# First FFN of a two-layer hybrid block on one core: the first tokens are transposed before they are normalised, and the token factor is applied later

## The chip, the core and the metric

The kernel runs on one core of a Trainium2 chip. The metric is the device time of one execution in microseconds (us), as the median of several runs. A core has five engines that run in parallel, each through its own list of instructions in a fixed order: TensorE (PE in the profile, its weight loads PEld), VectorE (DVE), ScalarE (ACT), GpSimd (POOL) and SyncE (SP), which here issues all DMA transfers. They wait for one another by semaphores. Matrix products land in PSUM, everything else lives in SBUF, and weights come from HBM.

## What is computed

The reference takes `x` (256 tokens of 1024 channels, float32) through two layers. Each layer has a feed-forward block at half weight, a mixer (a convolution with a state-space part, or attention) and another feed-forward block, each between two RMS norms. Only the beginning matters here:

```python
def rms_norm(x, g):
    y = x * lax.rsqrt(jnp.mean(x * x, axis=-1, keepdims=True) + NORM_EPS)
    return y * g

def swiglu(u, w1, w2):
    gate, up = jnp.split(u @ w1, 2, axis=-1)       # w1: 1024 x 5632
    return (jax.nn.silu(gate) * up) @ w2           # w2: 2816 x 1024

h = x
h = h + 0.5 * rms_norm(swiglu(rms_norm(h, g[0]), ffn_w1[0, 0], ffn_w2[0, 0]), g[1])
```

An RMS norm multiplies each token by one number (the token factor, from the mean square of its 1024 channels) and each channel by one weight (the norm weight `g`). Since both are plain factors, `(r * x * g) @ w` equals `r * ((x * g) @ w)` for each token.

## The kernel before, in words

**Precision by parts.** A float32 value is split into a high part, rounded to the type `fp32r`, which PE multiplies fast, and a low part, the remainder. A product of two such values is three PE products: high by high, high by low, low by high (`mm3`, line 646). Splitting takes one ScalarE instruction (the copy that rounds) and one VectorE instruction (the subtraction); weights are split on the chip too (`split`, line 613, and `prefetch`, line 617). In the profile `raw` is a weight unit as it was loaded (128 x 2048, 1 MB), `wh` and `wl` are its high and low part, made in pieces of 512 columns. Four units of each have room.

**The work of a feed-forward block** (`ffn`, line 830). The 2816 hidden channels are taken in 11 chunks of 256. The first two chunks are computed token-major (`gated_tok`, line 774): tokens are the rows of the result, so for each block of 128 tokens (t = 0, 1) the stationary side is x and the moving side 512 columns of weights (256 of the gate, 256 of the up half). The gate is then applied (`gate_mul`, line 803), and the hidden values are transposed. Chunks 2 to 10 are computed feature-major (`gated_feat`, line 811, with `by_parts`, line 682): here the stationary side is a block of weights and the moving side is the transposed x with all 256 tokens, high and low parts in one go. For both, x has to lie transposed in SBUF, channels on partitions, in eight blocks of 128 channels (`kb`). Between these, products with `w2` (`down`, line 846) are accumulated; those of chunks 0 and 1 stand behind chunk 2. A chunk of two units of weights takes PE 10.9 us.

**The beginning** (`run`, line 1356). SP loads the first token block in two halves, then an identity matrix, the first norm weights, the second token block in two halves, and weights. For each token block `post_pre` (line 738) takes the squares' sums on ScalarE, the token factor by `rstd` (line 726: VectorE and a power on GpSimd), multiplies the tokens by it on VectorE (`y` in the profile), transposes the result in eight 128 x 128 pieces on PE (`to_transposed`, line 704), and splits it while it copies it out of PSUM, where the norm weight is applied as well, which then stands one to a partition: four ScalarE copies with a scale, then four VectorE instructions for the low parts. The transposed x lies in the tiles `x`.

**What sets the order.** All instructions are first recorded (`Recorder`, line 252), each with a rank: its number in the recording, plus an offset (`moved`, line 315: -2000 for `post_pre`, -1950 for the splits of the first two weight units, +800 for later ones). Each carries what it depends on; of a PSUM tile the recorder also makes an instruction of one engine depend on the last user on another engine (`add`, line 277). `schedule` (line 340) then plays the program through with estimated costs and landing times, and takes on each engine, among the instructions that could start next, the one with the lowest rank. The order so found is written down, one list for each engine, and line 475 issues it: this is why nearly every row of the profile carries the line L475. On the chip the order is fixed; an engine waits at each instruction until its inputs are there.

PSUM has eight banks: four `a`, two `w`, one `t` and one `c`. Buffers in SBUF are named `s`, `cv`, `pt`, `sg`, `x` and so on, each with a fixed number of places.

Of the kernel before, what the change touches and what calls it, by code (L numbers as in the profile page):

```python
# [17 lines left out]
P = 128  # L18
D = 1024
DFF = 2816  # L20
SEQ = 256
NT = SEQ // P
KB = D // P
EPS = 1e-6
# [7 lines left out]
HURRY = 2000  # L32
# [130 lines left out]
N_CHAN = 340  # L163
# [86 lines left out]
class Recorder:  # L250
# [26 lines left out]
    def add(self, engine, name, args, kw):  # L277
        op = Op(len(self.ops), engine, name, args, kw)
        op.rank = op.index + self.offset
        self.ops.append(op)  # L280
        out = kw.get("out", args[0] if args else None)
        writes = (out, kw.get("accum_out"))
        views = [a for a in (*args, *kw.values()) if isinstance(a, View)]
        for a in sorted(views, key=lambda a: a in writes):
            self.touch(op, a, a in writes)
        for buf in op.bufs:
            if buf.kind.psum:
                own = engine in ("tensor", "vector") and any(w.buf is buf for w in writes if isinstance(w, View))
# [4 lines left out]
        op.cost, op.tail = cost(op, out)  # L293

    def touch(self, op, view, write):
        buf = view.buf
# [17 lines left out]
    @contextmanager  # L314
    def moved(self, ranks):

        before = self.offset
        self.offset += ranks
        yield
        self.offset = before  # L320

    @contextmanager
    def together(self):
# [16 lines left out]
    def schedule(self):  # L340
# [51 lines left out]
        while len(order) < len(ops):  # L392
# [9 lines left out]
            for b in o.bufs:  # L402
                if b.slot is None:
# [7 lines left out]
                    left[b] = len(b.uses)  # L411
                    b.last = 0.0
            length = o.cost
            if e == "scalar" and o.table:
                if o.table != table:
                    length += TABLE_LOAD
                table = o.table
# [64 lines left out]
GAP = 100.0  # L482
PAIRED = True
FIRST = 730.0
DMA_START = 1100.0
DMA_LATENCY = 900.0
LOOK = {"tensor": 50.0, "vector": 100.0, "scalar": 100.0, "gpsimd": 0.0, "sync": 0.0}
# [67 lines left out]
class Kernel:  # L555
    def __init__(self, ctx, tc, x, weights, w_dt, gains, chan, heads, dt_bias, consts, out):
        self.tc, self.nc = tc, Recorder(tc)
        self.weights, self.gains = weights, gains
        self.x, self.out = x, out
        self.n = 0  # L560
        self.next_unit = 0
        self.use_unit = 0
        self.units = {}
        self.bg = []
# [12 lines left out]
        self.ident = self.keep("ident", [P, P])  # L577
        self.order = self.keep("order", [P, 2, P])
# [4 lines left out]
        self.mean = self.keep("mean", [P, P])  # L583
        nc.gpsimd.memset(self.mean, 1.0 / D)
# [26 lines left out]


    def split(self, hi, lo, src, engine=None):
        self.nc.scalar.activation(hi, src, AF.Copy)
        (engine or self.nc.vector).tensor_tensor(out=lo, in0=src, in1=hi.bitcast(F32), op=ALU.subtract)

    def prefetch(self, upto):
# [36 lines left out]
        return [self.slot([P, 2, 2, SEQ], F32R, "x") for _ in range(KB // 2)]  # L654

    def xa(self, xT, t, kb):
        return tuple(xT[kb // 2][:, kb % 2, p, t * P : (t + 1) * P] for p in range(2))

    def xb(self, xT, kb):
# [114 lines left out]
    def gated_tok(self, xT, func, consume, bank="tt", first=False):  # L774
        nc = self.nc
        units = [[self.unit(512), self.unit(512)] for _ in range(2)]
        prods = {}
# [1 line left out]
        def product(t, c):  # L779
            ps = self.ps([P, 512])  # L780
            self.tok_major(ps, xT, t, units[c])
            prods[t, c] = self.gate_mul(ps, func)

        if first:
            ps = [self.ps([P, 512]) for _ in range(NT)]
            for part in range(2):
                for t in range(NT):
                    self.tok_major(ps[t], xT, t, units[0], range(part * 4, part * 4 + 4))
            for t in range(NT):
                prods[t, 0] = self.gate_mul(ps[t], func)  # L790
        else:
            product(0, 0)
        product(0, 1)
# [9 lines left out]
    def gate_mul(self, ps, func, out=None):  # L803
        if out is None:
            out = self.slot([P, 256], tag="pt")
        sg = self.slot([P, 256], tag="sg")
        self.nc.scalar.activation(sg, ps[:, 0:256], func)
        self.nc.vector.tensor_tensor(out=out, in0=sg, in1=ps[:, 256:512], op=ALU.mult)
        return out

    def gated_feat(self, xT, func, parts=None):
# [15 lines left out]
        return out  # L827


    def ffn(self, xT, done):  # L830
        nc = self.nc
        hid = {}

# [522 lines left out]
    def run(self):  # L1356
# [5 lines left out]
            (self.attention, False),  # L1362
            (self.ffn, True),
        ]
        xT = self.transposed_tile()
        load = self.nc.sync.dma_start
        for hf in range(2):
            c = slice(hf * 512, (hf + 1) * 512)
            load(out=self.h[0][:, c], in_=self.x[0:P, c])
        load(out=self.ident, in_=self.consts[:, C_ID : C_ID + P])  # L1370
        load(out=self.gain0, in_=self.in_small[0][:, N_CHAN : N_CHAN + KB])
        for hf in range(2):
            c = slice(hf * 512, (hf + 1) * 512)
            load(out=self.h[1][:, c], in_=self.x[P : 2 * P, c])
        self.prefetch(2)
        for t in range(NT):
            self.post_pre(t, None, False, None, self.gain0, xT)
        for i, (stage, half) in enumerate(stages):
            box = {}

# [8 lines left out]
            stage(xT, done)  # L1389
            xT = box["x"]  # L1390
        self.nc.issue()

# [44 lines left out]
```

## Time and profile before

| | before |
|---|---|
| median of 3 runs | 1077.49 us (1076.29 to 1078.73) |
| profiled execution, first to last instruction | 1074.9 us (its time is given by this span alone) |
| granted PE clock, mean | 0.998 |
| PE busy | 1058.9 us |
| VectorE busy | 762.3 us |
| ScalarE busy | 654.9 us |
| first weight piece landed | 8.23 us |
| first product of the first chunk | 9.20 us |

How to read it: times count from the first instruction of the profile. A row of the timeline gives start, duration, engine, line, operation, the tile written, an arrow and the tiles read, shapes, the number of merged instructions and, in brackets, how long the engine had been idle and what ended it. PE's records overlap, as one product starts before the one ahead has drained; the pace is read from the starts, not the durations. In the list of groups the second number behind the bar is the mean duration of one in ns. For DMA issues the last number is the time from issue to landing.

### The profile page before, as it was taken

How to read it: one execution, taken by the hardware profiler on the slowest of the kernel's cores; microseconds unless marked ns; L12 is line 12 of the kernel's file. 1: busy time of each engine (PE TensorE's matmuls, PEld its weight loads, DVE VectorE, ACT ScalarE, POOL GpSimd, SP SyncE). 2: the span in 40 equal slices, each digit the busy share in tenths (PEclk: the TensorE clock that was granted, in tenths of full speed). 3: DMA queues.
4: the chain of work that ended last, by engine and by line, in shares of the span. 5: the costliest groups of instructions: out<-in, count | busy, mean ns of one | idle time of the engine just before them, and what ended most of it. 6: DMA issues, size and time to landing. Idle time of an engine off the chain costs nothing.

```text
span 1074.9 us, 15876 instructions
## 1 busy us (share of the span) xinstructions
PE 1058.9 (99%) x5822; PEld 897.9 (84%) x5822; DVE 762.3 (71%) x1572; ACT 654.9 (61%) x1449; POOL 147.4 (14%) x140
## 2 busy tenths in 40 slices
PE   7999999999999999999999999999999999999997
PEld 5888888888878888888888888888888788888886
DVE  5756666799999885666677666668688868566663
ACT  7745555777776664655565646556576656465552
POOL 2000000169896000000000000000000500000000
PEclk9999999999999999999999999999999999999999
DMA  9765564545324575546537465454645235554621
GB/s 335 282 214 180 181 211 181 170 145 197 118 90 148 194 264 205 193 164 225 181 138 275 162 229 182 171 196 155 252 155 186 99 118 207 205 196 162 227 82 39
DMA packets 30638, 196.58 MB, mean 183 GB/s; under 512 B 3680, under 2 KB 4576, under 8 KB 8032
## 3 DMA queue, kind: packets, MB, share of 16 engines
q1 hardware_dynamic: 30560, 195.57, 51.9%
q8 instruction: 45, 0.74, 0.3%
q14 instruction: 33, 0.27, 0.1%
HBM read 194.51 MB, written 1.05 MB: 182 GB/s over the span
## 4 chain that ended last, share of the span: by engine, by line
PE 93%; DVE 3%; ACT 2%; DMA 0%; issue 0%; SPq 0%; DVEq 0%; POOLq 0%; POOL 0%; ACTq 0%
PE w L475 38%; PE a L475 32%; PE t L475 12%; PE c L475 12%; DVE c L475 2%; DVE t L475 1%; ACT wh L475 1%; DMA raw<-in_weights 0%; ACT junk L475 0%; DVE s L475 0%; ACT c L475 0%; ACT t L475 0%; SPq L475 0%; DVE m L475 0%; DVE h L475 0%
## 5 line engine op out<-in xcount | busy, mean ns | idle before, releaser
L475 DVE TENSOR_TENSOR wl<-raw,wh 128x512 fp32r<-128x512 f32 x640 | 411.4, 690 | 157.2 <-ACT wh L475 155.0
L475 ACT ACTIVATE wh<-raw 128x512 fp32r<-128x512 f32 x712 | 403.9, 625 | 194.8 <-PE a L475 78.9
L475 PE MATMUL w<-x,wh 128*128 128x512 f32 (+1 forms) x864 | 263.8, 364 | 0.9 <-DVE pt L475 0.7
L475 PE MATMUL a<-wh,s 128*128 128x512 f32 x800 | 253.0, 390 | 0.0
L475 PE MATMUL w<-x,wl 128*128 128x256 f32 x752 | 209.2, 278 | 0.0
L475 PEld LDWEIGHTS w<-x,wh 128*128 128x128 f32 x864 | 154.7, 188 | 28.2 <-DVE pt L475 1.0
L475 PEld LDWEIGHTS a<-wh,s 128*128 128x128 f32 x800 | 149.9, 188 | 33.2 <-ACT s L475 1.0
L475 PE MATMUL w<-wh,x 128*128 128x512 f32 x512 | 166.8, 400 | 1.0 <-ACT x L475 0.8
L475 PE MATMUL a<-wl,s 128*128 128x512 f32 x400 | 156.5, 391 | 0.0
L475 PEld LDWEIGHTS w<-x,wl 128*128 128x128 f32 x752 | 141.4, 188 | 1.9 <-issue 0.9
L475 POOL TENSOR_TENSOR m<-m,mhalf 128x1 f32<-128x1 f32 x28 | 18.1, 647 | 794.8 <-DVE m L475 794.7
L475 PE MATMUL t<-x,wh 128*128 128x512 f32 x336 | 117.1, 390 | 0.0
L475 PE MATMUL c<-x,wh 128*128 128x512 f32 x336 | 117.1, 390 | 0.0
L475 PEld LDWEIGHTS w<-wh,x 128*128 128x128 f32 x512 | 95.9, 189 | 21.6 <-ACT x L475 1.6
L475 PE MATMUL w<-wl,x 128*128 128x512 f32 x256 | 101.8, 400 | 0.0
L475 POOL TENSOR_TENSOR wl<-raw,wh 128x512 fp32r<-128x512 f32 x72 | 90.6, 1293 | 28.0 <-ACT wh L475 27.9
L475 PE MATMUL t<-x,wl 128*128 128x256 f32 x336 | 93.2, 277 | 0.0
L475 PE MATMUL c<-x,wl 128*128 128x256 f32 x336 | 93.1, 277 | 0.0
L475 PEld LDWEIGHTS a<-wl,s 128*128 128x128 f32 x400 | 75.1, 188 | 14.3
L475 DVE TENSOR_TENSOR sg<-w,sg 128x256 f32<-128x256 f32 x72 | 30.5, 424 | 75.4 <-ACT sg L475 74.1
L475 ACT ACTIVATE sg<-w 128x256 f32<-128x256 f32 x96 | 36.6, 382 | 77.0 <-PE w L475 77.0
L475 PEld LDWEIGHTS c<-x,wh 128*128 128x128 f32 x336 | 63.1, 188 | 13.5
(176 smaller groups left out, 1201.3 us busy)
## 6 DMA issues: line engine op xcount, KB each, us to landing
raw<-in_weights SPq DMA_DIRECT2D x176, 1024.0 KB, 4.8
g<-in_gains SPq DMA_DIRECT2D x11, 512.0 KB, 5.5
raw<-in_weights SPq DMA_DIRECT2D x8, 256.0 KB, 6.3
h<-in_x SPq DMA_DIRECT2D x4, 256.0 KB, 3.1
out<-h SPq DMA_DIRECT2D x4, 256.0 KB, 2.0
g<-in_consts SPq DMA_DIRECT2D x3, 192.0 KB, 2.3
chan<-in_chan SPq DMA_DIRECT2D x1, 170.0 KB, 8.7
order<-in_consts SPq DMA_DIRECT2D x1, 128.0 KB, 8.8
```

The lines of the kernel that those rows point to most:

```text
L475: o.ins = f(*[real(a) for a in o.args], **{k: real(a) for k, a in o.kw.items()})
```

## The change

The beginning of the kernel is rewritten; behind the first feed-forward block nothing differs.

- The identity is no longer loaded. GpSimd makes it (a clear, then a select on the diagonal). SP's order is now: first token block, norm weights, second token block, weights.
- PE runs four throw-away f32 products of the identity with itself, and then turns the raw tokens by f32 products with the identity, eight for each token block.
- The turned raw tokens are multiplied by the norm weights as they are copied out of PSUM and split into high and low parts, for the first four channel blocks of each token block by ScalarE, for the other four by one VectorE product. The token factor isn't in them. The second token block's parts depend, for the scheduler, on the first split of a weight piece.
- The two token-major chunks use these parts. Their gate applies the token factor: as a scale of the activation, and in the VectorE product.
- Behind these two chunks `scaled` makes the x for all others: each block's token factor is widened to 128 x 128 (ScalarE), turned by PE, copied out (ScalarE); VectorE adds high and low part, multiplies by the factors, and the result is split anew.
- The sums of squares move behind; they depend, for the scheduler, on the first load or on the fourth split.
- The scheduler counts PE instructions that start ahead of 6500 ns at twice their cost.

```diff
     def split(self, hi, lo, src, engine=None):
-        self.nc.scalar.activation(hi, src, AF.Copy)
+        self.splits.append(self.nc.scalar.activation(hi, src, AF.Copy))
...
+    def raw_turned(self, t, q, bank):
+        nc = self.nc
+        ps = self.ps([P, 4, P], bank)
+        for k in range(4):
+            kb = 4 * q + k
+            nc.tensor.matmul(ps[:, k, :], self.h[t][:, kb * P : (kb + 1) * P], self.ident, start=k == 0, stop=k == 3)
+        return ps
+
+    def raw_parts(self, t, q, ps):
+        nc = self.nc
+        hi, lo = (self.slot([P, 4, P], F32R) for _ in range(2))
+        gains = self.gain0[:, 4 * q : 4 * q + 4]
+        if q:
+            nc.vector.tensor_tensor(out=hi, in0=ps, in1=gains.unsqueeze(2).to_broadcast([P, 4, P]), op=ALU.mult)
+        for k in range(4):
+            if not q:
+                nc.scalar.activation(hi[:, k, :], ps[:, k, :], AF.Copy, scale=gains[:, k : k + 1])
+            nc.vector.scalar_tensor_tensor(out=lo[:, k, :], in0=ps[:, k, :], scalar=gains[:, k : k + 1], in1=hi[:, k, :].bitcast(F32), op0=ALU.mult, op1=ALU.subtract)
+        return hi, lo
+
+    def begin(self):
+        nc = self.nc
+        warm = self.ps([P, P])
+        raw, scale = {}, []
+        halves = [(t, q) for t in range(NT) for q in range(2)]
+        with nc.moved(-HURRY):
+            for _ in range(4):
+                nc.tensor.matmul(warm, self.ident, self.ident, start=True, stop=True)
+            ps = {(t, q): self.raw_turned(t, q, "tcaa"[2 * t + q]) for t, q in halves}
+            for q in range(2):
+                raw[0, q] = self.raw_parts(0, q, ps[0, q])
+        self.prefetch(2)
+        with nc.moved(-HURRY), nc.following(self.splits[0]):
+            for q in range(2):
+                raw[1, q] = self.raw_parts(1, q, ps[1, q])
+        for t in range(NT):
+            ss = self.sm(2)
+            with nc.following(self.splits[3] if t else self.loads[0]):
+                for hf in range(2):
+                    self.sumsq(ss[:, hf : hf + 1], self.h[t][:, hf * 512 : (hf + 1) * 512], 1 / 32.0)
+            scale.append(self.rstd(ss, EPS))
+        return raw, scale
+
+    def scaled(self, raw, scale):
+        nc = self.nc
+        V = nc.vector
+        over = self.slot([P, SEQ], tag="pt")
+        for t in range(NT):
+            wide = self.slot([P, P], tag="sg")
+            nc.scalar.activation(wide, scale[t].to_broadcast([P, P]), AF.Copy)
+            ps = self.ps([P, P], "c")
+            nc.tensor.transpose(ps, wide, self.ident)
+            nc.scalar.activation(over[:, t * P : (t + 1) * P], ps, AF.Copy)
+        xT = self.transposed_tile()
+        for (t, q), (hi, lo) in raw.items():
+            f = self.slot([P, 4, P], tag="cv")
+            V.tensor_tensor(out=f, in0=hi.bitcast(F32), in1=lo.bitcast(F32), op=ALU.add)
+            V.tensor_tensor(out=f, in0=f, in1=over[:, t * P : (t + 1) * P].unsqueeze(1).to_broadcast([P, 4, P]), op=ALU.mult)
+            to = self.x_out(xT, t)
+            for j in range(2):
+                self.split(*(part(2 * q + j) for part in to), f[:, 2 * j : 2 * j + 2, :])
+        return xT
...
     def ffn(self, xT, done, scale=None):
...
-        self.gated_tok(xT, AF.Silu, consume, first=self.use_unit == 0)
+        self.gated_tok(xT, AF.Silu, consume, scale=scale)
+        if scale:
+            xT = self.scaled(xT, scale)
...
+            self.nc.scalar.activation(sg, ps[:, 0:256], func, scale=scale)
+            self.nc.vector.scalar_tensor_tensor(out=out, in0=ps[:, 256:512], scalar=scale, in1=sg, op0=ALU.mult, op1=ALU.mult)
...
     def run(self):
...
-        load(out=self.ident, in_=self.consts[:, C_ID : C_ID + P])
...
-        for t in range(NT):
-            self.post_pre(t, None, False, None, self.gain0, xT)
+        xT, scale = self.begin()
```

`following(op)` makes every operation recorded inside it depend on `op` in the scheduler's books only.

More of the change, by code (lines that the diff above doesn't have):

```diff
@@ L293, in add @@
         op.cost, op.tail = cost(op, out)
+        return op
     def touch(self, op, view, write):
@@ L320, in moved, with following @@
         self.offset = before
+    @contextmanager
+    def following(self, op):
+        at = len(self.ops)
+        yield
+        for o in self.ops[at:]:
+            o.deps.setdefault(op.index, False)
     @contextmanager
@@ L413, in schedule @@
             length = o.cost
+            if e == "tensor" and s < COLD:
+                length *= 2
             if e == "scalar" and o.table:
@@ L484 @@
 FIRST = 730.0
+COLD = 6500.0
 DMA_START = 1100.0
@@ L563, in __init__ @@
         self.units = {}
-        self.bg = []
+        self.splits, self.loads = [], []
         nc = self.nc
@@ L577, in __init__ @@
         self.ident = self.keep("ident", [P, P])
+        nc.gpsimd.memset(self.ident, 0.0)
+        nc.gpsimd.affine_select(out=self.ident, in_=self.ident, pattern=[[-1, P]], compare_op=ALU.not_equal, fill=1.0, base=0, channel_multiplier=1)
         self.order = self.keep("order", [P, 2, P])
@@ L582, in __init__ @@
         nc.gpsimd.memset(self.mhalf, -0.5)
-        self.mean = self.keep("mean", [P, P])
-        nc.gpsimd.memset(self.mean, 1.0 / D)
         self.chan = self.keep("chan", [P, N_CHAN])
@@ L656, in xa @@
     def xa(self, xT, t, kb):
+        if isinstance(xT, dict):
+            return tuple(a[:, kb % 4, :] for a in xT[t, kb // 4])
         return tuple(xT[kb // 2][:, kb % 2, p, t * P : (t + 1) * P] for p in range(2))
@@ L771, in _post_pre, with gated_tok @@
         self.to_transposed(yg, *self.x_out(xT, t), KB, gain=gpre if y is None else None, later=0 if y is not None else SECOND)
-    def gated_tok(self, xT, func, consume, bank="tt", first=False):
+    def gated_tok(self, xT, func, consume, bank="tt", scale=None):
         nc = self.nc
@@ L781, in product @@
             self.tok_major(ps, xT, t, units[c])
-            prods[t, c] = self.gate_mul(ps, func)
-        if first:
+            prods[t, c] = self.gate_mul(ps, func, scale=scale and scale[t])
+        if scale:
             ps = [self.ps([P, 512]) for _ in range(NT)]
@@ L789, in gated_tok @@
             for t in range(NT):
-                prods[t, 0] = self.gate_mul(ps[t], func)
+                prods[t, 0] = self.gate_mul(ps[t], func, scale=scale[t])
         else:
@@ L801, in gated_tok, with gate_mul @@
             consume(c, pt.rearrange("p t b n -> p b t n"))
-    def gate_mul(self, ps, func, out=None):
+    def gate_mul(self, ps, func, out=None, scale=None):
         if out is None:
@@ L806, in gate_mul @@
         sg = self.slot([P, 256], tag="sg")
-        self.nc.scalar.activation(sg, ps[:, 0:256], func)
-        self.nc.vector.tensor_tensor(out=out, in0=sg, in1=ps[:, 256:512], op=ALU.mult)
+        if scale is None:
+            self.nc.scalar.activation(sg, ps[:, 0:256], func)
+            self.nc.vector.tensor_tensor(out=out, in0=sg, in1=ps[:, 256:512], op=ALU.mult)
+        else:
+            self.nc.scalar.activation(sg, ps[:, 0:256], func, scale=scale)
+            self.nc.vector.scalar_tensor_tensor(out=out, in0=ps[:, 256:512], scalar=scale, in1=sg, op0=ALU.mult, op1=ALU.mult)
         return out
@@ L827, in gated_feat, with ffn @@
         return out
-    def ffn(self, xT, done):
+    def ffn(self, xT, done, scale=None):
         nc = self.nc
@@ L841, in consume @@
             nc.vector.tensor_tensor(out=lo, in0=src, in1=hi.bitcast(F32), op=ALU.subtract)
-        self.gated_tok(xT, AF.Silu, consume, first=self.use_unit == 0)
+        self.gated_tok(xT, AF.Silu, consume, scale=scale)
+        if scale:
+            xT = self.scaled(xT, scale)
         acc = [None, None]
@@ L1364, in run @@
         ]
-        xT = self.transposed_tile()
         load = self.nc.sync.dma_start
-        for hf in range(2):
-            c = slice(hf * 512, (hf + 1) * 512)
-            load(out=self.h[0][:, c], in_=self.x[0:P, c])
-        load(out=self.ident, in_=self.consts[:, C_ID : C_ID + P])
[L1371 to L1375, printed above, removed]
-        for t in range(NT):
-            self.post_pre(t, None, False, None, self.gain0, xT)
+        for t in range(NT):
+            for hf in range(2):
+                c = slice(hf * 512, (hf + 1) * 512)
+                self.loads.append(load(out=self.h[t][:, c], in_=self.x[t * P : (t + 1) * P, c]))
+            if t == 0:
+                load(out=self.gain0, in_=self.in_small[0][:, N_CHAN : N_CHAN + KB])
+        xT, scale = self.begin()
         for i, (stage, half) in enumerate(stages):
@@ L1387, in done @@
                 self.post_pre(t, y, half, box["post"], box["pre"], box["x"], last=last)
-            stage(xT, done)
+            stage(xT, done, *([] if i else [scale]))
             xT = box["x"]
```

## The prediction

> **What bounds the kernel now.** I read the page first, then the chain of waits in order of time, then the timeline of the first 50 us engine by engine, then the groups by form for prices.
>
> ```profile
> span 1074.9 us, 15876 instructions
> PE 1058.9 (99%) x5822; PEld 897.9 (84%) x5822; DVE 762.3 (71%) x1572; ACT 654.9 (61%) x1449; POOL 147.4 (14%) x140
> ```
>
> TensorE (PE) is busy for 99% of the span; 16 us are idle. The change touches only the first stage, so what counts is where PE stands late there.
>
> ```profile
> 3.53 4.70 DMA raw<-in_weights
> ...
> 9.20 2.38 PE w L475 x4
> 11.58 0.85 PE t L475 x4
> 12.43 5.22 PE w L475 x22
> 17.65 0.44 PE c L475 x4
> 18.09 10.72 PE w L475 x46
> 28.82 0.44 PE t L475 x4
> 29.25 5.49 PE w L475 x24
> 34.75 0.22 PE t L475 x2
> 34.97 1.40 PE w L475 x8
> ```
>
> This is the chain (start, duration, what). The first weight piece lands at 8.23 and the first product starts at 9.20. After that the chain is PE alone. The "w" rows are the token-major products of the first two chunks: 4 + 22 + 46 + 24 = 96 (24 per token block and chunk). The last 24 take 5.49 us, 0.229 each, so 96 need 22.0. They stretch from 9.20 to 34.75, 25.55 us, in which 0.85 + 0.44 go to turning x and 0.44 to turning the first chunk's hidden values. So 25.55 - 1.73 - 22.0 = 1.8 us are lost, nearly all ahead of 12.43. Right behind, at 34.97, chunk 2 begins without a gap. I call the end of the fourth product E: 34.75 before.
>
> ```profile
> 9.19 0.29 PEld L475 LDWEIGHTS w<-wh,x 128*128 128x128 f32 x1 [1.24 <-ACT x L475]
> 12.23 0.86 PEld L475 LDWEIGHTS w<-wh,x 128*128 128x128 f32 x3
> 13.14 0.42 PEld L475 LDWEIGHTS w<-wl,x 128*128 128x128 f32 x2
> 6.39 1.12 PE L475 MATMUL t<-ident,y 128*128 128x128 f32 x4 [6.39 <-DVE y L475]
> ```
>
> Part of the 1.8 us is a slow PE: a weight load takes 0.29 us from 9.19 up to the three at 12.23, and 0.21 from 13.14 on; four turns at 6.39 take 1.12, the four at 28.82 take 0.44. The trace shows PE speeding up after some 4 us of work.
>
> **The change, part by part.**
>
> *The loads.* The identity's load goes. SP issues about 0.46 us apart, so the second half of h and the weights are issued 0.46 sooner, and the first piece lands at 7.8 instead of 8.23 (8.2 if bandwidth rather than issue sets it: the identity is only 64 KB). On GpSimd a clear and a select over 128x128 replace the load; they run while the first half of h is still on its way.
>
> ```profile
> 0.77 0.20 POOL L475 MEMSET mean<- 128x128 f32 x1
> 0.74 0.86 SPq L475 DMA_DIRECT2D h<-in_x  x2
> 3.33 0.63 ACT L475 ACTIVATE junk<-h 128x512 bf16<-128x512 f32 x1 [1.31 <-DMA h<-in_x]
> 7.47 0.63 ACT L475 ACTIVATE junk<-h 128x512 bf16<-128x512 f32 x1 [0.78 <-DMA h<-in_x]
> ```
>
> The trace has no select. By the clear it is 0.2 us, by a GpSimd pass over four times as many elements (5.06 / 4 = 1.27, below) at most that: identity ready by 2.5, ahead of h at 3.33. Cost nothing, on that cover.
>
> *The turns.* Four throw-away products and 16 f32 products replace 16 transposes. No f32 128x128 product stands here on its own; a slow transpose is 0.28, a fast one 0.11. Even at 0.45 the first eight end by 7.0. The second eight wait for the last half of h, which was read at 7.47, and end by 9 to 10.5. What remains of them may stand ahead of the first product (between 0 and 1 us); I put it in the next term.
>
> *The start of the products.* The normalising chain (square, power, scale) no longer stands ahead of x. If nothing else waits, the first product starts 0.13 after the first high part (7.8 + 0.63 = 8.4), at 8.5: 0.7 sooner, and the 1.8 lost and the 1.29 of turns leave the stretch: a gain of 3.8 us at most. But VectorE (DVE) must first make the low parts.
>
> ```profile
> 8.26 0.63 ACT L475 ACTIVATE wh<-raw 128x512 fp32r<-128x512 f32 x1
> 8.92 0.69 DVE L475 TENSOR_TENSOR wl<-raw,wh 128x512 fp32r<-128x512 f32 x1 [0.48 <-ACT wh L475]
> 9.95 1.13 DVE L475 SCALAR_TENSOR_TENSOR x<-t,gain,x 128x128 fp32r<-128x128 f32 x4
> 30.53 2.49 DVE L475 TENSOR_TENSOR wl<-raw,wh 128x512 fp32r<-128x512 f32 x4
> 13.69 5.06 POOL L475 TENSOR_TENSOR wl<-raw,wh 128x512 fp32r<-128x512 f32 x4 [4.56 <-ACT wh L475]
> ```
>
> The scheduler takes the lowest rank among what can start. Counting the recorded operations, the second token block's parts stand at ranks of about -1935 to -1923, the first unit's weight splits at -1905 to -1898: so the low weights queue behind them. And the recorder orders ScalarE and VectorE on one PSUM tile as recorded; as the new code records high, low, high, low for each 128 columns, the two engines alternate where before four highs ran and then four lows. Of 16 lows (0.28 each), some 14 are left at 8.4: 3.96, with one high on DVE 0.69, and four low weights 2.49: 7.1 us, to 15.5. Then the last 6 products of the first unit and 24 of the second, 30 x 0.229 = 6.9: the first chunk ends at 22.4. Before it ended at about 28.82 - 24 x 0.229 = 23.3. That is 0.9 gained. If the first token block's lows are all done by 8.4, six fewer, 1.7 more is gained, 2.6. I take 1.0, the order by rank; bounds: 3.8 gained, and 1.0 lost if ScalarE's split for the first token block also waits for weight pieces in fixed order.
>
> *The token factor in the first two chunks.* A scale on the activation and a scaled product instead of a plain one on DVE: the same count, the nearest row for both 0.42. Nothing.
>
> *The scaled x behind two chunks.* All of this is new, and it stands between the fourth product and chunk 2. The two turns of the widened factor are recorded behind the fourth product, whose steps are all ready, so PE takes them at E. They share one PSUM bank, so the second waits for the first copy. Only then can DVE multiply.
>
> ```profile
> 25.00:30.00 5.00, 5.00 (x25) 4.14 (x24) 2.22 (x6) 4.48 (x8) 0.00 (x0) 1.00 1.02 423
> 34.78 0.38 ACT L475 ACTIVATE sg<-w 128x256 f32<-128x256 f32 x1 [1.57 <-PE w L475]
> 35.82 0.41 DVE L475 TENSOR_TENSOR pt<-sg,w 128x256 f32<-128x256 f32 x1
> 37.40 0.69 DVE L475 TENSOR_TENSOR s<-t,s 128x512 fp32r<-128x512 f32 x1
> L475 DVE TENSOR_TENSOR x<-t,x 128x256 fp32r<-128x256 f32 x20 | 7.5, 417 | 0.0
> L475 ACT ACTIVATE x<-t,gain 128x128 fp32r<-128x128 f32 x8 | 2.4, 366 | 0.2 <-PE t L475 0.2
> ```
>
> From E: silu 0.38 and the first copy 0.3 on ScalarE, to E+0.75. DVE meanwhile has the gate product 0.41 (from E+0.5). Chunk 2's first product needs both token blocks of the first columns, high and low. In recorded order DVE has ahead of it: the gate product 0.41, three or four multiplies at 0.62 (2.49 / 4), five lows of 128x256 at 0.36 to 0.42, and the second chunk's hidden low 0.69: 0.41 + 2.49 + 1.9 + 0.6 = 5.4, from E+0.5 to E+5.9. The four sums of high and low need no factor and lie earlier, where DVE has room (2.22 us busy of 5, fourth column of times). Before, chunk 2 started at E+0.2. So 5.7 lost. What can PE do meanwhile? The hidden turns (0.44, done before too), and chunk 0's down products.
>
> ```profile
> 23.80 0.33 SPq L475 DMA_DIRECT2D raw<-in_weights  x1
> raw<-in_weights SPq DMA_DIRECT2D x1, 1024.0 KB, 6.3
> 38.00 1.28 DVE L475 TENSOR_TENSOR wl<-raw,wh 128x512 fp32r<-128x512 f32 x2
> 39.54 1.28 DVE L475 TENSOR_TENSOR wl<-raw,wh 128x512 fp32r<-128x512 f32 x2
> 46.37 0.40 PE L475 MATMUL a<-wh,s 128*128 128x512 f32 x1
> ```
>
> Their weights (the seventh unit) are issued at 23.80 and land at 30.1, but their splits carry a rank raised by 800, behind every scaled operation, and their buffer comes free only in the middle of the fourth product. High halves may be there: two to four products at 0.229, 0.5 to 0.9. I credit 0.7: **5.0 lost**. Bounds: 2.5, if the first token block's factor is turned before E (left: one multiply, one high, one low and their waits, E+2.7); 7.5, if the four low weights of chunk 2's second unit (2.49) come in between.
>
> *DVE and ScalarE later.* The 5 us of DVE work push back the seventh unit's split. It was done at 40.82 and first used at 46.37: 5.5 us of cover, which moves along with PE. Nothing; without the cover, up to the shortfall. Behind 50 us PE is full in both, so what is lost or won at the start reaches the end one to one.
>
> **Sum.** Median 1077.49; the profiled execution's span is 1074.9, 2.6 below, and I add differences to the median. 1077.5 - 1.0 + 5.0 = **1081.5**.
>
> A rule speaks against such a stall. In the Trainium skill, "TensorE: Matmul & The Clock Gate", section "HAM oscillation", an idle PE of more than about 3.4 us falls back to half its clock; no row here shows it, since PE never idles as long once it has begun. By it the forecast would turn into the rival "slow PE" below.
>
> **The rivals.**
>
> *Stall filled.* PE's order is fixed by the scheduler's own estimates of landings and costs. If by these the factor is turned in a gap of PE ahead of E for both blocks, or the down products are placed in the stall (24 x 0.229 = 5.5, just its length), chunk 2 starts within 0.3 of E plus useful work. With the start clean: 1077.5 - 3.8 + 0.5 = 1074.2; with a gain of 2.6 at the start, 1075.4. For it: 24 such products exist. Against: the rank of the splits, and a fourth product with no gap. This decides the sign: it needs both a clean start and a filled stall.
>
> *Half hidden.* The first block's factor slips into a PE gap during the third product (there is one: the gate ahead of it ran late).
>
> ```profile
> 20.85 1.28 ACT L475 ACT_TABLE_LOAD   x1
> 22.14 0.38 ACT L475 ACTIVATE sg<-w 128x256 f32<-128x256 f32 x1
> ```
>
> Then 2.5 is lost at E, and with 1.0 to 3.8 gained the time is 1076.2 to 1079.0: no change by 0.2%, which is 2.2 us and about what a measurement of this kernel can tell.
>
> *Slow PE.* The stall lets PE fall to its first speed again. From 9.19 to 13.14 loads took 0.29 instead of 0.21: over 3.95 us, 1.1 us lost by the loads, 2.0 if the products ran at half speed: 1082.6 to 1083.5. For it: nearly 4 idle us between the hidden turns (E+1.6) and E+5.5. Against: a few products may fall into it.
>
> *Start no better.* The queue on DVE eats the whole start: 1077.5 + 5.0 = 1082.5, in the forecast's own range.
>
> **How the numbers follow.** Forecast with its start variants 0.47, slow PE 0.10, half hidden 0.24, stall filled 0.19. Slower by over 0.2%: forecast and slow PE, with a little of half hidden, 0.59; same 0.23; faster 0.18. The forecast's own range is 1079.1 (3.8 gained, 5.4 lost) to 1083.5 (none gained, 6.0 lost). The whole range goes down into the filled case, 1074.9, leaving out some 0.13 below, and up to 1083.8, leaving out 0.06.
>
> **What would show it.** Right: PE products at a steady 0.23 from about 8.5 to 12 on, loads at 0.19 from the first product; two turns into bank c right behind the fourth product; then an idle PE of 4 to 5 us whose releaser is a DVE product into x, with DVE full. The first chunk's end near 22.4 tests the start. Wrong: no PE gap ahead of chunk 2, or "a" products in it; the first factor turned before E; the first chunk ending by 20; weight loads of 0.29 behind the stall (slow PE).

## The result and the profile after

| | before | after |
|---|---|---|
| median (5 runs each) | 1077.87 us (1076.29 to 1078.84) | 1083.99 us (1082.61 to 1084.98) |
| ratio, 95% interval | | 1.0061 (1.005 to 1.0072) |
| profiled execution: time, span | span 1074.9 us | 1084.24 us, span 1082.4 us |
| mean granted clock | 0.998 | 0.996 |

The change makes the kernel 6.1 us slower by the medians. The direction was forecast; the time lies 0.2 us above the range's upper end and 2.5 us above the forecast. In each run whose time and span are both known the time is 1.7 to 1.9 us over the span. An estimate from this is that the profiled run of before took about 1076.7 us (1074.9 + 1.8), 1.2 below its median: the two spans differ by 7.5 us, more than the medians do. One run of e9_all_warm below took 1322.06 us at a mean granted clock of 0.752, and it enters no comparison.

The first lines of the page of after, and the row of the granted clock in 40 slices of 27 us:

```profile
span 1082.4 us, 15942 instructions
...
PE 1066.3 (99%) x5848; PEld 903.2 (83%) x5848; DVE 772.1 (71%) x1586; ACT 656.1 (61%) x1453; POOL 149.6 (14%) x141
...
PEclk9899999999999999999999999999999999999999
```

PE is still busy for 99% of a longer span. What stands out on the page is the 8 in the second slice of PEclk, from 27 to 54 us. The chain of waits of after (start, duration, what):

```profile
3.06 5.44 DMA raw<-in_weights
...
9.19 0.69 DVE wl L486
9.88 2.42 DVE s L486 x8
...
12.90 1.55 DVE s L486 x6
14.45 0.61 DVE wl L486
...
15.11 1.66 PE w L486 x6
...
16.81 12.12 PE w L486 x52
28.92 0.44 PE t L486 x4
29.36 2.53 PE w L486 x11
...
36.28 0.40 DVE pt L486
36.67 1.80 DVE cv L486 x3
38.48 0.60 DVE s L486
39.08 1.68 DVE x L486 x5
...
40.90 8.52 PE w L486 x32
```

In before this chain was PE alone from 9.20 on. Now VectorE carries it twice: from 9.19 to 15, where the low parts of the weights (`wl`) and of the turned x (`s`) stand in one queue, and from 36.28 to 40.76, where gate product, three multiplies (`cv`), the hidden values' low part (`s`) and five low parts (`x`) follow one another. Behind that the 32 products of chunk 2 take 8.52 us, 0.27 each. The timeline of PE in after shows the second place:

```profile
34.67 0.38 PE L486 MATMUL t<-ident,pt 128*128 128x128 f32 x2
34.89 0.27 PE L486 MATMUL c<-ident,sg 128*128 128x128 f32 x1
35.95 0.33 PE L486 MATMUL c<-ident,sg 128*128 128x128 f32 x1 [0.79 <-ACT pt L486]
36.73 0.44 PE L486 MATMUL t<-ident,pt 128*128 128x128 f32 x2 [0.45 <-DVE pt L486]
37.16 1.25 PE L486 MATMUL a<-wh,s 128*128 128x512 f32 x4
40.90 0.76 PE L486 MATMUL w<-x,wh 128*128 128x512 f32 x1 [2.48 <-DVE x L486]
```

The rows of before for the same place:

```profile
34.59 0.38 PE L475 MATMUL t<-ident,pt 128*128 128x128 f32 x2
34.72 0.47 PE L475 MATMUL w<-x,wh 128*128 128x512 f32 x1
```

In after both turns of the factor stand right behind the fourth product, the second waits for the copy out of the bank that they share, four down products (`a`) follow, and chunk 2 waits for VectorE until 40.90 (34.72 in before). ScalarE had the widened factors long before PE turned them:

```profile
23.92 0.30 ACT L486 ACTIVATE sg<-m 128x128 f32<-128x128 f32 x1
...
25.16 0.29 ACT L486 ACTIVATE sg<-m 128x128 f32<-128x128 f32 x1
```

So the first factor was ready from 24.2 on, and what held its turn back to 34.89 was its place in PE's written order; the second turn follows the first through their bank. The windows of after (busy us of PE, PEld, DVE, ACT, POOL, then the granted clock, DMA share and GB/s), and three weight loads from the timeline of PEld, show what the wait does to PE:

```profile
37.00:41.00 4.00, 1.52 (x7) 0.73 (x5) 4.00 (x10) 4.00 (x12) 0.00 (x0) 0.87 0.40 168
41.00:46.60 5.60, 5.60 (x18) 4.73 (x19) 4.97 (x10) 2.68 (x6) 0.00 (x0) 0.50 0.55 190
46.60:52.00 5.40, 5.40 (x32) 4.76 (x31) 2.98 (x6) 1.19 (x3) 0.00 (x0) 0.98 0.59 200
```

```profile
40.87 0.29 PEld L486 LDWEIGHTS w<-x,wh 128*128 128x128 f32 x1 [2.89 <-issue]
...
46.16 0.33 PEld L486 LDWEIGHTS w<-x,wl 128*128 128x128 f32 x1
...
46.79 0.19 PEld L486 LDWEIGHTS w<-x,wl 128*128 128x128 f32 x1
```

For 5.6 us the granted clock is exactly 0.50, and PE issues 18 products there against 32 in the 5.4 us that follow. In the window ahead the mean is 0.87: if the clock fell once and stayed down, it fell 0.13 x 4 / 0.5 = 1.0 us before 41.0, at 40.0, and chunk 2 began at half speed. Finer windows agree: the mean is 0.95 from 39.5 to 40.0 and 0.50 from 40.0 on, and it is back at 1.00 from 46.8.

By the two profiles the 7.5 us add up like this: fourth product 0.1 later (its hidden turns start at 34.67 instead of 34.59); chunk 2's wait 6.1, less the four down products (4 x 0.229 = 0.9) and the two hidden turns (0.4) that lie in it, 4.8; half clock 2.7 (up to 46.6 the pairs of chunk 2's products start 0.64 apart where they took 0.35 in before: 9 pairs at 0.29 more make 2.6, and an experiment below gives 2.7 for the same 32 products). That is 7.6.

### The profile page after: what moved, and what is told of

It reads as the page before. It is cut to its first block, busy times and chain, and to the rows that moved or that the text cites. A ratio compares the mean times of both kernels' runs of the same rounds, so it can differ in the third digit from the quotient of the medians.

```text
span 1082.4 us, 15942 instructions
## 1 busy us (share of the span) xinstructions
PE 1066.3 (99%) x5848; PEld 903.2 (83%) x5848; DVE 772.1 (71%) x1586; ACT 656.1 (61%) x1453; POOL 149.6 (14%) x141
## 4 chain that ended last, share of the span: by engine, by line
PE 92%; DVE 5%; ACT 2%; DMA 1%; issue 0%; SPq 0%; DVEq 0%; POOLq 0%; POOL 0%; ACTq 0%
PE w L486 37%; PE a L486 31%; PE t L486 12%; PE c L486 11%; DVE c L486 1%; DVE t L486 1%; ACT wh L486 1%; DVE s L486 1%; DVE wl L486 1%; DMA raw<-in_weights 1%; ACT junk L486 0%; DVE cv L486 0%; ACT c L486 0%; ACT t L486 0%; SPq L486 0%
## 5 line engine op out<-in xcount | busy, mean ns | idle before, releaser
L486 PE MATMUL w<-wh,x 128*128 128x512 f32 x448 | 145.5, 398 | 0.1
L486 PEld LDWEIGHTS w<-wh,x 128*128 128x128 f32 x448 | 83.6, 188 | 17.3 <-issue 1.0
L486 PE MATMUL w<-wl,x 128*128 128x512 f32 x224 | 88.8, 398 | 0.0
```

The costliest lines, as they stand in the source:

```text
L486: o.ins = f(*[real(a) for a in o.args], **{k: real(a) for k, a in o.kw.items()})
```

## The experiments

Each was timed beside before on the same chip, with 5 runs (e1, e3, e4, e11) or 11; the medians of before were 1077.69 us (beside e1 to e4), 1077.74 (e5 to e8) and 1077.27 (e9 to e11). The last three ran on another chip than the first eight. My theory once the result was known: the wait ahead of chunk 2 costs 4 to 5 us by itself, the clock that falls in it another 2, and the new start earns nothing because VectorE's queue eats it. The rivals: that the wait costs it all and the clock only shows (then a PE kept busy would gain nothing), or that the beginning itself is worse.

**PE kept busy in the wait (e1_busy).** Sixteen products, whose results go nowhere, are put behind the turns of the factor.

```diff
         xT = self.transposed_tile()
+        idle = self.ps([P, 4, P])
+        for _ in range(16):
+            nc.tensor.matmul(idle, raw[0, 0][0][:, 0, :], raw[0, 0][0], start=True, stop=True)
```

> Sixteen throw-away products (128x512, high parts of the raw x, result unused) are added on PE between the turn of the factor and chunk 2, 16 x 0.23 = 3.7 us of PE work where PE stood idle. Nothing else changes, so chunk 2 still waits for VectorE until about 40.9. Theory (idle PE falls to half clock and chunk 2 pays for it, 2.6 us): granted clock stays at 1.00 from 41 to 47, weight loads at 0.19, time 2 to 3 us below the changed kernel's 1084, so 1081 to 1082. Rival (the clock falls for another reason, such as the f32 products at the start or the load of all engines together): clock 0.5 as before, time 1084.

Measured: 1081.77 us (1081.48 to 1082.6), ratio to before 1.0042 (1.003 to 1.0055). The chain and the window of e1_busy that answer to the last rows above:

```profile
39.52 1.69 DVE x L486 x5
...
41.34 5.84 PE w L486 x32
```

```profile
41.00:46.60 5.60, 5.26 (x30) 4.66 (x31) 5.60 (x12) 3.52 (x8) 0.00 (x0) 1.00 0.52 167
```

Chunk 2 begins no sooner, still behind VectorE's low parts (41.34; the weights landed 0.4 later in this profile), but the clock stays at 1.00 and the same 32 products take 5.84 us instead of 8.52. A PE that does useless work makes the kernel 2.2 us faster than after. So the fall of the clock is a cost of its own, and an idle PE is what brings it about; what is left, 4.1 us over before, is the wait.

**Half as much (e11_half_busy).** The same with 7 products for 16, to see how short an idle time is short enough.

> The changed kernel with seven throw-away products instead of sixteen in the stall: PE is busy up to about 38.5 and then idle for 2.3 to 2.9 us, as long as the last idle stretch of the changed kernel (2.93). Theory (the clock falls after some 3.4 us of little PE work taken together, not from the last 2.9 us alone): clock 1.00 in chunk 2, 1081.5 to 1082. Rival (the last idle stretch alone makes it fall): clock 0.5 up to 44 or 47, 1083 to 1084.

Measured: 1082.45 us (1081.52 to 1083.17), ratio 1.0045 (1.0033 to 1.0058), between the two. The windows of e11_half_busy:

```profile
37.00:41.00 4.00, 1.64 (x7) 0.78 (x6) 4.00 (x10) 4.00 (x11) 0.00 (x0) 0.99 0.46 193
41.00:46.60 5.60, 5.49 (x23) 4.78 (x24) 5.19 (x10) 2.90 (x7) 0.00 (x0) 0.71 0.47 180
```

In this profile the clock fell at about 40.9, 2.3 us behind the last product, and chunk 2's pairs are 0.64 apart up to 44.2. Two of the five runs have a mean clock of 0.997 (1082.97, the profiled one, and 1083.17 us), three 0.999 (1081.52 to 1082.45). That reads as an idle time at the edge, where the clock falls in some runs and not in others; five runs don't show where the edge is, and it stays open. By PE's rows the last stretch without a product is 2.47 us here and 2.48 in after (the expectation put it at 2.93), so its length alone doesn't decide; what differs is that PE had no gap from 35.0 to 38.0 here.

**The factor turned early (e2_early_factor).** The turns of the factor go to the front, where ScalarE has it ready, and the rest of `scaled` stays ahead of the later splits. Two tiles get places of their own, since the old places come free too late.

```diff
-        over = self.slot([P, SEQ], tag="pt")
-        for t in range(NT):
+        over = self.slot([P, 512], tag="y0")
+        with nc.moved(-HURRY):
+            for t in range(NT):
...
-        for (t, q), (hi, lo) in raw.items():
+        with nc.moved(640):
+            for (t, q), (hi, lo) in raw.items():
```

> The same work as the changed kernel, but the factor is widened, turned and copied as soon as it is there (rank -2000, buffers y0 and y1 of their own instead of pt and sg), and the sums, multiplies and splits of the scaled x get rank +640, behind the weight splits of units 3 and 4 and ahead of the later ones. The start is untouched. Theory (all of the loss is the wait ahead of chunk 2 and the clock that falls in it; the start gains nothing): chunk 2 follows the fourth product within 0.5 us, clock 1.00, the first chunk still ends at 22.9 to 23.2, time 1076.5 to 1078.5, the kernel before's. Rival (8 us more work on VectorE costs PE time wherever it stands): a wait of 2 to 5 us turns up in the third or fourth product or in chunk 2, time 1080 to 1083.

Measured: 1077.32 us (1076.74 to 1077.77), ratio 0.9997 (0.9989 to 1.0006). The chain and one window of e2_early_factor:

```profile
28.44 6.70 PE w L486 x29
35.14 0.22 PE t L486 x2
35.36 1.41 PE w L486 x8
```

```profile
23.00:34.60 11.60, 11.60 (x54) 9.22 (x53) 11.29 (x23) 10.95 (x23) 0.00 (x0) 1.00 0.80 304
```

Chunk 2 follows the fourth product without a gap, as in before; VectorE takes the multiplies and splits into the stretch ahead, where it is now busy for 11.29 of 11.60 us (8.71 in after). The whole loss is gone: the time is 6.6 us below that of e3_no_warm (below), which is level with after and ran on the same chip. So the loss was the wait and what came with it; any other cost of the change lies within the noise. The run moves the turns and gives the scaled x a rank of its own at the same time, so what each is worth alone isn't shown. But the change so mended is no faster than before either: the new start by itself is worth -0.4 us, with an interval of about -1.2 to +0.6.

**Without the throw-away products (e3_no_warm).** The four products of the identity with itself are left out.

```diff
-            for _ in range(4):
-                nc.tensor.matmul(warm, self.ident, self.ident, start=True, stop=True)
```

> The changed kernel without its four throw-away products of the identity. Theory (the start waits for VectorE's low parts, not for PE): the turns take longer (0.4 instead of 0.23 for the later ones), the first chunk's end moves by less than 0.5 us, time 1084 to 1084.6. Rival (a warm PE is what the start's gain depends on): the first products at 0.29 a load up to 12 or 13 us, first chunk's end 1 to 2 us later, time 1085 to 1086.

Measured: 1083.96 us (1083.25 to 1084.03), ratio 1.0061 (1.0048 to 1.0075): no difference from after, whose ratio is 1.0061. Weight loads took 0.19 from the first product on here too. So the 16 f32 products that turn x warm PE enough, and the four add nothing. The profile has the half clock again (mean 0.70 from 41.0 to 46.6), but for 3.4 us, from 41.4 to 44.8, where it was 6.8 in after:

```profile
41.10 7.30 PE w L486 x32
```

The 32 products of chunk 2 took 8.52 us in after and 5.84 in e1_busy. So the fall's price differs from run to run: 2.7 us in the profile of after, 1.5 in this one.

**Another order at the start (e4_start_order).** ScalarE's four copies ahead of VectorE's four low parts, as it was in before, and the low parts of the first weights ahead of the second token block's parts.

```diff
-FIRST_RANKS = (-1950, -1950)
+FIRST_RANKS = (-2030, -2030)
...
+        for k in range(4):
             nc.vector.scalar_tensor_tensor(out=lo[:, k, :], in0=ps[:, k, :], scalar=gains[:, k : k + 1], in1=hi[:, k, :].bitcast(F32), op0=ALU.mult, op1=ALU.subtract)
```

> The changed kernel with another order at the start: the four highs of a PSUM tile are recorded ahead of its four lows, and the splits of the first two weight units get rank -2030 instead of -1950, ahead of the second token block's parts. The scaled x is untouched. Theory (the low weights queue behind the lows of x on VectorE): the first chunk ends 1.5 to 2.5 us sooner, at 20.5 to 21.5; the wait ahead of chunk 2 and the half clock stay; time 1081.5 to 1082.5. Rival (the start is set by the landing of the weights or by PE's clock): first chunk's end near 22.9, time 1084.

Measured: 1082.67 us (1082.18 to 1083.1), ratio 1.0049 (1.0036 to 1.0062), 1.3 us below e3_no_warm on the same chip, with no overlap of the runs. (e3_no_warm stands in for after, whose ratio it has; the intervals of the ratios of after and of this run overlap a little.) The chain of e4_start_order:

```profile
11.36 8.27 PE w L486 x34
...
19.70 1.28 ACT L486
...
28.27 5.47 PE w L486 x24
33.74 0.22 PE t L486 x2
```

PE now runs from 11.36 on, and the hidden turns behind the fourth product start at 33.58 by the timeline (33.74 in the chain), 1.1 sooner than in after (34.67). VectorE's queue was what held the start. A new piece is late next: the ScalarE table for the gate is loaded at 19.70, only when the first gate asks for it, and PE waits 0.4 us behind it. A wait ahead of chunk 2 and the half clock (0.50 from 37.0 to 41.0, 0.75 up to 46.6) stay, so it stays slower than before; here the wait ends otherwise, as PE is idle for 3.16 us until ScalarE's splits let the four down products start at 38.81, and chunk 2 follows them at 40.69.

**Both mends together (e5_both)**, e2_early_factor with e4_start_order.

> Both corrections together: the factor turned early with rank +640 for the scaled x, and the start in the other order (four highs, then four lows; weight splits at rank -2030). Theory (the stall with its clock, and the queue on VectorE at the start, are separate and add up): 1077.3 of the early factor minus the 1.3 of the start order, 1075.5 to 1076.5, 0.1 to 0.2% below the kernel before. Rival (the time won at the start is lost again because VectorE is full up to chunk 2, 10.7 us busy of 11 in the early-factor run): waits in the third or fourth product, 1077 to 1078.

Measured: 1077.88 us (1077.25 to 1079.39), ratio 1.0005 (0.9996 to 1.0014). This fell: I had added up the two gains. A window of e5_both, and a stretch of its chain:

```profile
11.00:15.00 4.00, 4.00 (x11) 2.80 (x10) 4.00 (x12) 3.34 (x9) 2.23 (x2) 0.57 1.04 420
```

```profile
11.43 3.91 PE w L486 x9
...
26.94 0.60 DVE cv L486
27.54 0.62 DVE wl L486
...
28.20 1.43 PE w L486 x5
```

The clock is 0.57 from 11 to 15: nine products take 3.91 us, 0.43 each instead of 0.229, 1.8 us lost. PE had stood idle between its turns of x and the first product, from 8.2 to 9.5, and the clock fell at 11.6, 2 us after the products had begun; that the idle stretch is the cause is argued, not shown. The 1.8 us are just what the fourth product ends later than in e4_start_order (hidden turns at 35.57 instead of 33.74). The third product also waits on VectorE up to 28.20, which now has an early multiply between the weights' low parts; that costs PE little, 0.2 us (busy for 11.36 of 11.60 us from 23.0 on). So in this one run the half clock ate the start's gain. Its 11 runs have mean clocks of 0.997 (two) to 0.999 with no order in the times, so why the others are no faster stays open.

**The table loaded at the start (e6_both_table, e10_early_table).** One activation on a column of constants loads the gate's table while nothing else is on ScalarE. e6_both_table is e5_both with it, e10_early_table is e2_early_factor with it.

```diff
+        nc.scalar.activation(self.keep("early", [P, 1]), self.mhalf, AF.Silu)
```

> The run with both corrections, and ScalarE's table for the silu asked for by a 128x1 activation as its first instruction, so that the load of 1.28 us doesn't stand between the first chunk's product and its gate. In the start-order run PE waited 0.4 us there for the gate product. Theory: that wait goes, 0.4 to 0.8 us below the run with both corrections, about 1075. Rival (the gate isn't late because of the table): equal to it.

> The early factor and the early table, without the other order at the start. It separates what the order at the start is worth once the stall is gone. Theory (the order is worth 1.3 us also here): about 1077, 0.8 or more above the run with both and the table. Rival (the table gave all of it): 1076.2 as that run.

Measured: e6_both_table 1076.23 us (1075.76 to 1077.01), ratio 0.9988 (0.9979 to 0.9997); e10_early_table 1077.29 us (1076.39 to 1077.76), ratio 0.9998 (0.9989 to 1.0007). On e5_both the table brings 1.65 us, on the same chip and with no overlap of the runs, where 0.4 to 0.8 was expected. Where the rest comes from isn't shown: the one profile of e6_both_table is of its slowest run, in which PE waits for GpSimd's weight splits:

```profile
20.27 0.50 PE L486 MATMUL w<-wl,s 128*128 128x512 f32 x1 [0.78 <-POOL wl L486]
```

There the fourth product ends no sooner than in before (hidden turns at 34.59 in both). The table alone brings e2_early_factor nothing (0.9997 without). With both, the start's order is worth about 0.0010, 1.1 us, close to the 1.3 of e4_start_order, though the two intervals overlap and the runs were made on different chips.

**Before with parts of the new start (e7_before_warm, e8_before_table).** The old kernel with the identity made on chip and 18 throw-away products ahead, so that PE is warm; and the old kernel with the early table.

```diff
+        nc.gpsimd.memset(self.ident, 0.0)
+        nc.gpsimd.affine_select(out=self.ident, in_=self.ident, pattern=[[-1, P]], compare_op=ALU.not_equal, fill=1.0, base=0, channel_multiplier=1)
...
-        load(out=self.ident, in_=self.consts[:, C_ID : C_ID + P])
...
+        warm = self.ps([P, P])
+        with self.nc.moved(-HURRY):
+            for _ in range(18):
+                self.nc.tensor.matmul(warm, self.ident, self.ident, start=True, stop=True)
```

> The kernel before with one part of the change alone: the identity is made on the chip and 18 throw-away f32 products of it run on PE from 1.4 us, up to the first turn. Theory of the prediction (part of the 1.8 us lost in the first chunk is a PE at half speed): weight loads at 0.19 from the first product on, first chunk's end 0.5 to 1.5 us sooner, time 1076.3 to 1077.3. Rival (the first products wait for their operands, the speed doesn't matter): 1077.7, no change.

> The kernel before with the early request of the silu table alone, so that a gain of the run with both corrections and the table can be put to its cause. Theory: the 0.35 us that PE waited at 23.0 for the first gate goes, time 1077.2 to 1077.6. Rival (the scheduler's order on ScalarE keeps the gate late in any case): 1077.7.

Measured: e7_before_warm 1077.24 us (1075.34 to 1078.14), ratio 0.9995 (0.9986 to 1.0004); e8_before_table 1077.16 us (1075.48 to 1077.92), ratio 0.9996 (0.9986 to 1.0005). Neither can be told from no change. In e7_before_warm's profile the loads take 0.19 from the first product and its fourth product ends 0.44 sooner than before's (hidden turns at 34.31), so half a microsecond may be there. Its six runs with a mean clock of 0.997 took 1077.24 to 1078.14 us and its five with 0.998 or 0.999 took 1075.34 to 1076.86: a PE warmed early, that then waits for weights, seems to lose the clock again in about half of the runs. No profile shows one of the six, so that is a reading of the numbers only.

**Warm up to the first product (e9_all_warm).** e6_both_table with four more products of the identity, behind the turns of x, where e5_both's PE lay idle.

```diff
             ps = {(t, q): self.raw_turned(t, q, "tcaa"[2 * t + q]) for t, q in halves}
+            for _ in range(4):
+                nc.tensor.matmul(warm, self.ident, self.ident, start=True, stop=True)
```

> The run with both corrections and the early table, and four more throw-away products of the identity behind the turns, where PE otherwise stands idle for about a microsecond until the first weights. In the run with both corrections the clock fell in just this place (0.86 granted from 8 to 13, 0.90 from 13 to 23). Theory (the rest of the start's gain is lost to that clock): granted clock 1.00 from 8 to 23, 0.5 to 1.5 us below the 1076.2 of the run with both and the table. Rival (VectorE is what the third product waits for, whatever the clock): 1076 to 1076.5.

Measured: 1075.31 us (ten runs from 1074.54 to 1075.95), ratio 0.998 (0.9971 to 0.9989): 2.0 us faster than before and some 8.7 faster than after, by the two ratios. A window and the chain of e9_all_warm:

```profile
8.00:13.00 5.00, 4.62 (x26) 3.30 (x25) 3.84 (x9) 4.41 (x12) 0.48 (x1) 1.00 1.01 376
```

```profile
27.55 5.95 PE w L486 x26
33.50 0.22 PE t L486 x2
33.72 1.64 PE w L486 x9
```

The clock is 1.00 where e5_both's fell, and in every window up to 52 us; PE is busy for 4.62 of the 5 us in which the products begin, the useless ones included (3.30 in after, 4.16 in before), and chunk 2 begins behind the fourth product's hidden turns at 33.72, where before began it at 34.97. That a half clock avoided is what the four products gain isn't shown: the profile of e6_both_table reads 1.00 from 8 to 23 us without them, and the step from it to this run is 0.9 us by ratios whose intervals overlap, on different chips. PE's wait for GpSimd at 20.27 there has no counterpart here. This is the fastest version, and it beats both kernels: the idea of the change, with the factor turned early, VectorE's queue in another order, the table loaded ahead and PE kept busy up to the first weights.

## Why the prediction missed its range

*The size of the wait was right.* Forecast: chunk 2 ready at E + 5.9, less 0.2 and 0.7 of down products, 5.0 lost. Measured: E at about 34.67 in the timeline, chunk 2 at 40.90, E + 6.2; four down products, at the upper end of the two to four foreseen (the prediction also names such products as a sign of being wrong, against its own sum); 4.8 lost by the profile, and 4.4 between e1_busy and e2_early_factor. The steps were as put: two turns right behind the fourth product, the second behind the first's copy, three multiplies, five low parts of x and one of the hidden values, all on VectorE. The gate product began 1.0 later than put, at E + 1.5, behind seven low parts of weights that VectorE had begun at 31.97 and that the sum had not placed there (its bound of 7.5 had four of them); the queue behind it then took 4.6 instead of 5.4, as only three multiplies were ahead and the low parts were short.

*The step that failed: "Slow PE" as a rival with a chance of 0.10.* The sum had no term for a half clock behind the wait, so it stood there at nothing. I had counted "a few products may fall into it" against the half clock. Four did, from 37.16 to 38.4, and the clock fell 1.6 us behind them all the same. The sign that the prediction named for it stands in the rows: loads of 0.33 behind the wait. It is worth 2.2 us by e1_busy (1.5 and 2.7 in single profiles); all five runs of after have a mean clock of 0.996 or 0.997, and before's runs beside the experiments 0.998 or more, so it seems to come with every run. Its price was nearly right (1.1 to 2.0 from the start's loads). It should have stood in the forecast: the wait that the forecast itself put at nearly 4 idle us was the condition of the rival. The Trainium skill, "TensorE: Matmul & The Clock Gate", Part 1, says that the clock is halved after an idle window of about 3.4 us and restored after a busy one, and that the windows run freely, so that the point differs between runs. The rows agree on the half (0.50) and on the length: from fall to return it lasts 3.4 us in e3_no_warm, e5_both and e11_half_busy, and 6.8, twice that, in after and e4_start_order. They don't bear out the forecast's use of 3.4 us as a length that an idle stretch must have without a break, since here the clock fell 1.6 and 2.3 us behind the last of a few scattered products (after and e11_half_busy): in the 3.4 us ahead of the fall PE was still busy for 1.7 us in after, 1.2 in e11_half_busy, 0.9 in e3_no_warm and 1.9 in e5_both.

*The other step that failed: the start, -1.0.* Measured +0.1 by the profiles, -0.4 by e2_early_factor. The part of it that was wrong is the landing: "issued 0.46 sooner, and the first piece lands at 7.8". The weights were issued at 3.06 instead of 3.53 and landed at 8.50 instead of 8.23; in the other kernels that issue them at 3.06 between 8.39 and 9.29. Why, no run shows. It isn't only the identity's 64 KB, for then it would still have been a little sooner. The queue on VectorE was right, in kind and nearly in size: alternating with the second block's low parts, the low weights ended the wait at 15.1 to 16.8 (forecast 15.5), and e4_start_order, which takes that queue away, gains 1.3 us. The first chunk ends at about 23.3 (its last product starts at 23.07) instead of 22.4, later by roughly what the landing was. The prediction also misread where it ended in before: counted back from 28.82 it came to 23.3, but its last product starts there at 22.72, so it ended at about 22.95, and PE then waited 0.35 us for the first gate. So 22.4 would have been a gain of 0.55 at that point, not 0.9; after is 0.35 later there, but has no such wait.

*Right as forecast.* The identity on chip costs nothing (clear and select done at 1.3 us), weight loads take 0.19 from the first product (for the slow PE of before the loads are the sound sign; the prediction's four turns of 1.12 and 0.44 come from two views, and the timeline has 0.60 for the second), the factor in the two first chunks' gates costs nothing that any run shows (its instructions are longer, 0.47 instead of 0.38 on ScalarE and 0.48 instead of 0.41 on VectorE, but e2_early_factor has them and is level with before), and later stages pass the loss on one to one. "Stall filled" was the mechanism of e2_early_factor; its price (1074.2 to 1075.4) needed a clean start as well, and e9_all_warm, which has both, is at 1075.31. The sign was decided as that rival had put it.

In sum: -1.0 + 5.0 was forecast, and -0.4 + 4.4 + 2.2 = 6.2 measured by the experiments, against 6.1 by the medians.

## What to carry to other kernels

Work that is moved off the front of a kernel lands on some engine's queue further on: find where that engine has room and where the instruction that starts it stands in the written order, because a result ready at 25 us is worth nothing if its 0.2 us turn stands at 35. A wait of a TensorE that is otherwise full costs more than its length: here 4.4 us of waiting drew 2.2 us of half clock behind it, also with a few products scattered in it, so the price belongs in the sum when PE will have little work for some 3.4 us (here 0.9 to 1.9 us of it), and useless products are a quick way to measure it. Where several mends each look small, test them together too: e5_both gave nothing until the table was loaded early as well.

## What the runs showed of the hardware

The clock column does not show everything: in before it reads 1.00 from 8 to 13 us although loads take 0.29 there, while a fall later on is shown as 0.50. The slow PE at the very start is read from the loads alone.

VectorE and GpSimd were slow together. Four sums of two SBUF tiles on VectorE, the first two of them while GpSimd split weights, from the timelines of after:

```profile
16.80 4.56 DVE L486 TENSOR_TENSOR cv<-s,s 128x512 f32<-128x512 f32 x4
```

```profile
13.04 6.56 POOL L486 TENSOR_TENSOR wl<-raw,wh 128x512 fp32r<-128x512 f32 x4 [7.26 <-ACT wh L486]
```

By narrower windows the first two sums take about 1.7 us each and the other two 0.6 each, and GpSimd's splits take 1.64 each where it was 1.27 in before. The ends alternate: GpSimd at 17.86 and 19.60, VectorE 0.6 us behind each, at 18.46 and 20.15. The Trainium skill, "SBUF — State Buffer", section "SBUF: two separate sides", has the two engines take turns for a port, a whole instruction at a time, when VectorE reads two SBUF tiles; the longer times of both agree with it. None of these eight stands in the chain of after. But PE waited until 16.81, about 0.2 us, for one more, the low part of weights that VectorE began at 15.22: it took 1.53 us beside GpSimd where others take 0.69. No run measured the cost by itself.
